# First stage of a hybrid block: x sums in other tiles, normed parts ahead of adds, two splits and two constants moved

## The chip, the cores and the metric

The kernel runs on one core of a Trainium2 chip. The metric is the device time of one execution in microseconds (us). Engines are named as in the profile: PE (TensorE, the matmuls), PEld (its weight loads), DVE (VectorE), ACT (ScalarE), POOL (GpSimd) and SP (SyncE, which here issues most DMAs). Each engine works through its own list of instructions in order, and waits on semaphores for the others. L93 is line 93 of the kernel.

## What is computed

x is 1024 tokens by 1024 channels in float32. A mixer with two branches is followed by a SwiGLU block. Only the second branch is touched by the change:

```python
h = rms_norm(x, norm_mix_g[l])
proj = h @ w_in[l]
rnn_x, rnn_gate, sgu_u, sgu_v, gate_a, gate_b = jnp.split(proj, SPLIT_POINTS, axis=-1)
...
y_b = chunked_sgu(jax.nn.gelu(sgu_u), jax.nn.gelu(sgu_v), sgu_ln_g[l], sgu_ln_b[l], sgu_ws[l], sgu_bs[l])
```

`chunked_sgu` takes a layer norm of gelu(v) over its 1024 channels, multiplies each chunk of 128 tokens by a lower triangular 128x128 matrix for each of 8 groups of channels (the mixing), and multiplies the result by gelu(u). The first branch needs a few constants from `rg_lambda` (8 columns of 128) before its recurrence can run.

## The kernel before

Every float32 product is made of three matmuls with halves of the operands: ACT copies a value into a high half (`split`, L93), DVE subtracts to get the low half (L94), and PE adds hi*hi, hi*lo and lo*hi (L97, L98, L99). The large products are Strassen/Winograd products: seven block products M1 to M7, whose left operands are blocks of x or sums of them (A11, A12, A22, S1 to S4), each split once, and whose right operands are weights loaded to `wraw` and split (b11, b21, b22, and t1 to t4, which are sums formed on DVE by L206 to L217).

The first stage is the projection v with what hangs on it. Its instructions stand on every engine in the order in which the code is written (`tc.manual_schedule`, L554), up to `ms.__exit__`; behind that a scheduler of the framework orders them. Inside, the second half of v's columns runs in a loop over eight tiles t of 128 tokens. For each t, PE forms the tile (24 matmuls); `v_stats` applies gelu on ACT (L648) and takes statistics on DVE (L649, L653); when t closes its norm group (the groups are tile 0, tiles 1 and 2, 3 and 4, 5 and 6, and 7), `v_norm` forms 1/std on DVE (L659 and L390 to L399) and `v_centre` subtracts the mean on ACT (L668). The tile two places behind is then split into its normed parts (`v_split`: hi on ACT L674, lo on DVE L675; the tag `vn` has two buffers), mixed (`v_mix`: PE L686 and L687, then ACT copies the first sum to `mt`, L689; the tag `mt` has four buffers, four are used for each tile), and `v_mixed` adds the two sums on DVE (L695) and stores from `mt` to `mix_d`.

Between these stand the operands for the next products. `sums(i)` forms S1, the block for S3 and the one for S2 in place with three DVE operations over 128x1024 (L540, L541, L542); `sum_s4(i)` forms S4 (L545); `part(name, src, i)` splits half i of an operand, one ACT and one DVE instruction over 128x1024.

After the loop the two products u0 and u1 begin ("heads", one block product at a time, in the order M1, M2, M5, M6, M3, M7, M4), with the mixing of tiles 6 and 7, the splits of S2 and S4 and, by `take`, results evacuated late. Behind the written order, u's results are multiplied by the mixing's (L838 scales and shifts `mix`, L839 applies gelu to u, L841 multiplies), S3 and A22 are split, and u0 and u1 run to their end. Then come the constants of the recurrence (`sp_e`, L869 and L870; the exponential needs another activation table, ACT_TABLE_LOAD) and the products r0, r1, ... of the first branch mixed with u2, u3 and the gates.

Of the kernel before, what the change touches and what calls it, by code (L numbers as in the profile page):

```python
# [8 lines left out]
F32 = mybir.dt.float32  # L9
F32R = mybir.dt.float32r  # L10
I32 = mybir.dt.int32
AF = mybir.ActivationFunctionType
ALU = mybir.AluOpType

P = 128
T = 1024
D = 1024
NT = T // P
NK = D // P
HALF = 512  # L20
# [26 lines left out]
def ts(t):  # L47
    return slice(t * P, (t + 1) * P)
# [3 lines left out]
def block_kernel(ctx: ExitStack, tc: tile.TileContext, a: dict, out: bass.AP):  # L52
    nc = tc.nc
    act, dve, pool, pe = nc.scalar, nc.vector, nc.gpsimd, nc.tensor
# [30 lines left out]
    def ps(name):  # L85
        return psum.tile([P, HALF], F32, name=name, tag="ps")

    def slot(name, shape=(P, 4, 2, HALF), dt=F32R):
        return slots.tile(list(shape), dt, name=name, tag="s")

    def split(hi, lo, src, eng=None):

        act.activation(hi, src, AF.Copy)  # L93
        (eng or dve).tensor_sub(lo, src, hi.bitcast(F32))  # L94
# [14 lines left out]
    def tick():  # L109
        clock[0] += 1  # L110
        for fn in due.pop(clock[0], []):
            fn()
# [240 lines left out]
    for m in DOWN:  # L353
        i = DL[LEFT[m]]
# [57 lines left out]
    def tm_half(acc, name, A, t, ks, free=0, inner={}):  # L412


        for k in ks:
            w = weight((name, k))
            x = A[t // 4][k // 4][:, k % 4, :, ts(t % 4)]
            mm3(acc, x[:, 0], x[:, 1], w[:, 0], w[:, 1], k == 0, k == NK - 1)
            if k < free:
                allow(state["limit"] + 1)  # L420
            if k in inner:
                inner[k]()
# [26 lines left out]
    with tc.tile_pool(name="phv", bufs=1) as wk:  # L449
        ws = wk.tile([P, GROUPS, 2, P], F32R, name="ws")  # L450
        shift = wk.tile([P, GROUPS, P], F32, name="shift", tag="shift")
# [8 lines left out]
        s1s = {}  # L460
# [42 lines left out]
        def scale_x(h, ks):  # L503
            for k in ks:
                dve.scalar_tensor_tensor(F[h][:, k], F[h][:, k], par("mix_g", k), R[h], ALU.mult, ALU.mult)
# [22 lines left out]
        def part(name, src, i):  # L528

            ks = slice(2 * i, 2 * i + 2)  # L530
            if name not in ops:
                ops[name] = slot(f"h_{name}")
            split(ops[name][:, ks, 0], ops[name][:, ks, 1], src)

        def block(h, kh, i):
            return F[h][:, 4 * kh + 2 * i:4 * kh + 2 * i + 2]

        def sums(i):
            s1 = s1s[i] = wk.tile([P, 2, HALF], F32, name=f"xs{i}", tag="shift")
            dve.tensor_add(s1, block(1, 0, i), block(1, 1, i))  # L540
            dve.tensor_sub(block(1, 0, i), block(0, 0, i), block(1, 0, i))  # L541
            dve.tensor_sub(block(0, 0, i), s1, block(0, 0, i))  # L542

        def sum_s4(i):
            dve.tensor_sub(block(0, 1, i), block(0, 1, i), block(0, 0, i))  # L545
# [95 lines left out]
        v1, stats, mvs, vn, mts = {}, {}, {}, {}, {}  # L641
# [4 lines left out]
        def v_stats(t, acc):  # L646
            v1[t] = wk.tile([P, HALF], F32, name=f"vb{t}", tag="vb", bufs=3)
            act.activation(v1[t], acc, AF.Gelu_apprx_tanh, scale=rms[:, t:t + 1])  # L648
            dve.bn_stats(sts[t][:, 1], v1[t])  # L649
            g = group[t]  # L650
            if t == g[0]:
                mvs[t] = wk.tile([P, 3, len(g)], F32, name=f"mv{t}", tag=f"bnmv{len(g)}", bufs=2)
            dve.bn_aggr(mvs[g[0]][:, :2, t - g[0]], sts[t])  # L653

        def v_norm(t):

            g = group[t]
            mv = mvs[g[0]]
            dve.tensor_scalar(mv[:, 2], mv[:, 0], -1.0, None, ALU.mult)  # L659
            y = rstd_early(wk, mv[:, 1], 1.0, f"rv{t}", len(g))  # L660
            for j, u in enumerate(g):
                stats[u] = y[:, j:j + 1]

        def v_centre(t):
            g = group[t]
            for j, u in enumerate(g):
                for src in (v0[u], v1[u]):
                    act.activation(src, src, AF.Identity, bias=mvs[g[0]][:, 2, j:j + 1])  # L668

        def v_split(t):  # L670
            vn[t] = []
            for q, src in enumerate((v0[t], v1[t])):
                x = wk.tile([P, 2, HALF], F32R, name=f"vn{t}{q}", tag="vn", bufs=2)
                act.activation(x[:, 0], src, AF.Identity, scale=stats[t])  # L674
                dve.scalar_tensor_tensor(x[:, 1], src, stats[t], x[:, 0].bitcast(F32), ALU.mult, ALU.subtract)  # L675
                vn[t].append(x)

        def v_mix(t):
            mts[t] = []
            for i in range(4):  # L680
                g = 2 * i
                x = vn[t][i // 2]
                mx = ps(f"mx{t}{i}").rearrange("p (j s t) -> p j s t", j=2, s=2)
                for j in range(2):
                    c = ts((g + j) % 4)
                    pe.matmul(mx[:, j], x[:, 0, c], ws[:, g + j], start=True, stop=False, skip_group_check=True)  # L686
                    pe.matmul(mx[:, j, 0], x[:, 1, c], ws[:, g + j, 0], start=False, stop=True, skip_group_check=True)  # L687
                mt = wk.tile([P, 2, P], F32, name=f"mt{t}{i}", tag="mt", bufs=4)
                act.activation(mt, mx[:, :, 1], AF.Copy)  # L689
                mts[t].append((mt, mx))  # L690

        def v_mixed(t):
            for i, (mt, mx) in enumerate(mts.pop(t)):
                g = 2 * i
                dve.tensor_add(mt, mt, mx[:, :, 0])  # L695
                nc.sync.dma_start(mix_d[i // 2][:, g % 4:g % 4 + 2, ts(t)], mt)

        for t in range(NT):
            acc = ps(f"pv1{t}")
            if t == 0:  # L700
                state["limit"] = 2 * NK
            tm_half(acc, "wv1", H, t, range(NK), free=2 * (t == NT - 1))
            if t > 1:
                v_split(t - 2)
            if t < 2:
                scale_x(1, range(4 * t, 4 * t + 4))
            if 1 <= t < 3:
                part("A11", block(0, 0, t - 1), t - 1)
            if t == 2:
                sums(0)  # L710
            if t == 4:
                part("S1", s1s[0], 0)
                sums(1)
            if t == 5:
                part("S1", s1s[1], 1)
                part("A12", block(0, 1, 0), 0)
            if t == 6:
                part("A12", block(0, 1, 1), 1)
                sum_s4(0)
            if t == 7:  # L720
                sum_s4(1)
            v_stats(t, acc)
            if t == group[t][-1]:
                v_norm(t)
            if t > 1:
                v_mix(t - 2)
                v_mixed(t - 2)
            if t == group[t][-1]:
                v_centre(t)
            tick()  # L730
# [13 lines left out]
        def head(n):  # L744
            next(U[n])
            tick()

        def take(n):
            for fn in postponed[:n]:
                fn()  # L750
            del postponed[:n]

        cur["defer"] = True
        v_split(6)
        head("u0")
        v_mix(6)
        v_mixed(6)
        v_split(7)
        head("u1")
        take(2)  # L760
        head("u0")
# [9 lines left out]
        take(2)  # L771
        part("S4", block(0, 1, 1), 1)
        head("u0")
        head("u1")
        take(2)
        cur["defer"] = False
    ms.__exit__(None, None, None)

    with tc.tile_pool(name="phr", bufs=2) as wk:
# [70 lines left out]
        for fn in results:  # L850
            fn()
        results.clear()
        for i in range(2):
            part("S3", block(1, 0, i), i)
        for i in range(2):
            c = wk.tile([P, 2, HALF], F32, name=f"a22_{i}", tag="rr")
            act.activation(c, block(1, 1, i), AF.Copy)
            s1s[i] = c
        for i in range(2):
            part("A22", s1s[i], i)  # L860
        state["ahead"] = 5
        run(U["u0"], U["u1"])

# [2 lines left out]
        lam = wk.tile([P, 8], F32, name="lam", bufs=1)  # L866
        load(lam, a["lam"])
        sp = {n: wk.tile([P, 8], F32, name=f"sp_{n}", bufs=1) for n in ("e", "z", "z2", "p", "m", "c4", "c8")}
        act.activation(sp["e"], lam, AF.Abs)  # L869
        act.activation(sp["e"], sp["e"], AF.Exp, scale=-1.0)  # L870
        dve.tensor_scalar(sp["z"], sp["e"], 2.0, None, ALU.add)
        dve.reciprocal(sp["z"], sp["z"])
# [448 lines left out]
    for n, m in enumerate(DOWN):  # L1321
        c = m in CHAIN
# [97 lines left out]
```

## Time and profile before

| | |
|---|---|
| three runs, us | 1429.61, 1430.56, 1432.44; median 1430.56 |
| profiled execution, us | 1431.23 |
| its span, us, and mean granted clock | 1429.5; 0.993 |
| instructions | 17233 |
| busy in the span | PE 98%, PEld 81%, DVE 77%, ACT 56%, POOL 5% |

The profiled execution is one run, with its span measured from the first to the last instruction. Times of a row are microseconds from the span's start. A row of a timeline gives the start, the duration, the engine, the line, the operation, what it writes and reads by the program's names, and in brackets how long the engine was idle just before and what ended that. The granted clock is the share of full speed that PE was given.

### The profile page before, as it was taken

The numbers are of one execution on the slowest core, as the hardware profiler recorded it, in microseconds if no ns is written. First come the engines' busy times: TensorE is split into PE (matmuls) and PEld (weight loads), VectorE is DVE, ScalarE is ACT, GpSimd is POOL, SyncE is SP. The second block draws the span as 40 slices with busy tenths as digits, with TensorE's granted clock in tenths as the row PEclk, the third lists the DMA queues.
The fourth block names the chain that finished last, engine by engine and source line by source line (L and its number), as shares of the span: only waits on it lengthen the run. The fifth ranks groups of instructions, "written<-read, shape, count | busy, mean of one in ns | idle before, by whom it ended". The sixth has DMA issues, their size and how long they took to land.

```text
span 1429.5 us, 17233 instructions
## 1 busy us (share of the span) xinstructions
PE 1403.3 (98%) x6216; PEld 1154.9 (81%) x6216; DVE 1097.7 (77%) x1807; ACT 794.0 (56%) x1320; POOL 74.7 (5%) x59
## 2 busy tenths in 40 slices
PE   9998999999999999999999999999999999999997
PEld 7877887788888887788888788888888888888886
DVE  7998999988888887689757776666666665697585
ACT  8467688888889974353443533333333333444454
POOL 0000000000000000000000021111111111000000
PEclk9999999999999999999999999999999999999999
DMA  9323545433333387773611122222322226842342
GB/s 321 137 60 106 203 160 180 168 116 114 114 121 101 109 327 285 262 291 129 220 60 44 74 111 110 111 92 101 110 111 111 96 96 254 331 182 94 110 141 81
DMA packets 73349, 212.45 MB, mean 149 GB/s; under 512 B 6576, under 2 KB 20912, under 8 KB 60720
## 3 DMA queue, kind: packets, MB, share of 16 engines
q1 hardware_dynamic: 73120, 211.32, 41.5%
q8 instruction: 48, 0.79, 0.2%
q14 instruction: 37, 0.30, 0.1%
q10 hardware_dynamic: 144, 0.04, 0.0%
HBM read 148.68 MB, written 62.65 MB: 148 GB/s over the span
## 4 chain that ended last, share of the span: by engine, by line
PE 71%; DVE 12%; ACT 8%; DMA 5%; issue 2%; SPq 1%; DVEq 0%; ACTq 0%; POOLq 0%; POOL 0%
PE f_p L97 10%; PE f_p L99 10%; PE f_p L98 10%; PE d_M L98 5%; PE d_M L99 5%; PE d_M L97 5%; PE g_p L99 2%; PE g_p L98 2%; PE g_p L97 2%; PE po L97 2%; PE po L99 2%; PE po L98 2%; DMA sb<-sgb_d 2%; PE pa_p L97 2%; PE pa_p L98 2%
## 5 line engine op out<-in xcount | busy, mean ns | idle before, releaser
L93 ACT ACTIVATE dl_M<-wraw 128x512 fp32r<-128x512 f32 x77 | 48.6, 631 | 105.0 <-PE d_M L99 92.2
L98 PE MATMUL d_M<-d_M,dl_M 128*128 128x512 f32 x264 | 102.8, 389 | 0.0
L97 PE MATMUL d_M<-d_M,dl_M 128*128 128x512 f32 x264 | 102.7, 389 | 0.0
L99 PE MATMUL d_M<-d_M,dl_M 128*128 128x512 f32 x264 | 102.7, 389 | 0.0
L93 ACT ACTIVATE f_t<-wraw 128x512 fp32r<-128x512 f32 x88 | 55.5, 630 | 84.0 <-PE f_p L99 71.3
L94 DVE TENSOR_TENSOR dl_M<-wraw,dl_M 128x512 fp32r<-128x512 f32 x77 | 54.0, 701 | 51.5 <-ACT dl_M L93 51.3
L94 DVE TENSOR_TENSOR f_t<-wraw,f_t 128x512 fp32r<-128x512 f32 x88 | 71.7, 815 | 23.6 <-ACT f_t L93 22.6
L97 PE MATMUL f_p<-m,f_b 128*128 128x512 f32 x176 | 69.1, 393 | 0.0
L98 PE MATMUL f_p<-m,f_b 128*128 128x512 f32 x176 | 68.9, 392 | 0.0
L99 PE MATMUL f_p<-m,f_b 128*128 128x512 f32 x176 | 68.9, 391 | 0.0
L97 PE MATMUL f_p<-f_S,f_t 128*128 128x512 f32 x176 | 68.5, 389 | 0.0
L98 PE MATMUL f_p<-f_S,f_t 128*128 128x512 f32 x176 | 68.5, 389 | 0.0
L99 PE MATMUL f_p<-f_S,f_t 128*128 128x512 f32 x176 | 68.5, 389 | 0.0
L97 PE MATMUL f_p<-m,f_t 128*128 128x512 f32 x176 | 68.5, 389 | 0.0
L98 PE MATMUL f_p<-m,f_t 128*128 128x512 f32 x176 | 68.5, 389 | 0.0
L99 PE MATMUL f_p<-m,f_t 128*128 128x512 f32 x176 | 68.5, 389 | 0.0
L93 ACT ACTIVATE f_b<-wraw 128x512 fp32r<-128x512 f32 x66 | 41.1, 626 | 36.2 <-PE f_p L99 31.8
L94 DVE TENSOR_TENSOR f_b<-wraw,f_b 128x512 fp32r<-128x512 f32 x66 | 45.4, 687 | 18.8 <-ACT f_b L93 18.1
L98 PEld LDWEIGHTS d_M<-d_M,dl_M 128*128 128x128 f32 x264 | 49.5, 188 | 10.5 <-DVE d_M L94 0.2
L97 PEld LDWEIGHTS d_M<-d_M,dl_M 128*128 128x128 f32 x264 | 49.6, 188 | 10.4
L99 PEld LDWEIGHTS d_M<-d_M,dl_M 128*128 128x128 f32 x264 | 49.6, 188 | 10.1
L206 DVE TENSOR_TENSOR wraw<-wraw 128x512 f32<-128x512 f32 x50 | 53.0, 1060 | 1.0
(506 smaller groups left out, 4219.7 us busy)
## 6 DMA issues: line engine op xcount, KB each, us to landing
wraw<-in_w_gu_dram SPq DMA_DIRECT2D x22, 1024.0 KB, 4.9
wd<-in_w_down_dram SPq DMA_DIRECT2D x11, 1024.0 KB, 8.7
wraw<-in_w_r_dram SPq DMA_DIRECT2D x8, 1024.0 KB, 6.4
wraw<-in_w_g_dram SPq DMA_DIRECT2D x8, 1024.0 KB, 5.0
wraw<-ffs_d SPq DMA_DIRECT2D x8, 1024.0 KB, 5.0
wraw<-ffa_d SPq DMA_DIRECT2D x6, 1024.0 KB, 6.1
xn<-in_x_dram SPq DMA_DIRECT2D x8, 512.0 KB, 9.2
wraw<-in_w_u_dram SPq DMA_DIRECT2D x4, 1024.0 KB, 5.6
```

What stands on the lines that cost most here:

```text
L93: act.activation(hi, src, AF.Copy)
L94: (eng or dve).tensor_sub(lo, src, hi.bitcast(F32))
L97: pe.matmul(o, lh, rh, start=start, stop=False, **kw)
L98: pe.matmul(o, lh, rl, start=False, stop=False, **kw)
L99: pe.matmul(o, ll, rh, start=False, stop=stop, **kw)
L206: dve.tensor_sub(b11, b12, b11)
```

## The change

In the loop, `sums(0)` and `sums(1)` move from tiles 2 and 4 to tiles 3 and 5; the splits of S1 and A12 are made at tiles 4 and 6; `sum_s4(0)` moves from tile 6 to 7, and `sum_s4(1)` behind the mixing of tile 6. The normed parts of tile 6 are made between the mixing of tile 5 and its adds, those of tile 7 between the mixing of tile 6 and its adds. The splits of S3, the copies of A22's block and their splits move from behind the written order into its end, with buffers of other tags. The first operation of the recurrence constants is bound to its place in the program's order.

```diff
--- before.py
+++ after.py
@@ -706,24 +706,22 @@
                 scale_x(1, range(4 * t, 4 * t + 4))
             if 1 <= t < 3:
                 part("A11", block(0, 0, t - 1), t - 1)
-            if t == 2:
-                sums(0)
-            if t == 4:
-                part("S1", s1s[0], 0)
-                sums(1)
-            if t == 5:
-                part("S1", s1s[1], 1)
-                part("A12", block(0, 1, 0), 0)
-            if t == 6:
-                part("A12", block(0, 1, 1), 1)
+
+            if t in (3, 5):
+                sums(t // 4)
+            if t in (4, 6):
+                i = t // 2 - 2
+                part("S1", s1s[i], i)
+                part("A12", block(0, 1, i), i)
+            if t == 7:
                 sum_s4(0)
-            if t == 7:
-                sum_s4(1)
             v_stats(t, acc)
             if t == group[t][-1]:
                 v_norm(t)
             if t > 1:
                 v_mix(t - 2)
+                if t == NT - 1:
+                    v_split(6)
                 v_mixed(t - 2)
             if t == group[t][-1]:
                 v_centre(t)
@@ -751,11 +749,11 @@
             del postponed[:n]
 
         cur["defer"] = True
-        v_split(6)
         head("u0")
         v_mix(6)
+        v_split(7)
         v_mixed(6)
-        v_split(7)
+        sum_s4(1)
         head("u1")
         take(2)
         head("u0")
@@ -771,8 +769,15 @@
         take(2)
         part("S4", block(0, 1, 1), 1)
         head("u0")
+        a22 = [wk.tile([P, 2, HALF], F32, name=f"a22_{i}", tag=("shift", "vn")[i], bufs=1 + i) for i in range(2)]
+        for i in range(2):
+            act.activation(a22[i], block(1, 1, i), AF.Copy)
+        part("S3", block(1, 0, 0), 0)
         head("u1")
+        part("S3", block(1, 0, 1), 1)
         take(2)
+        for i in range(2):
+            part("A22", a22[i], i)
         cur["defer"] = False
     ms.__exit__(None, None, None)
 
@@ -850,14 +855,6 @@
         for fn in results:
             fn()
         results.clear()
-        for i in range(2):
-            part("S3", block(1, 0, i), i)
-        for i in range(2):
-            c = wk.tile([P, 2, HALF], F32, name=f"a22_{i}", tag="rr")
-            act.activation(c, block(1, 1, i), AF.Copy)
-            s1s[i] = c
-        for i in range(2):
-            part("A22", s1s[i], i)
         state["ahead"] = 5
         run(U["u0"], U["u1"])
 
@@ -866,7 +863,8 @@
         lam = wk.tile([P, 8], F32, name="lam", bufs=1)
         load(lam, a["lam"])
         sp = {n: wk.tile([P, 8], F32, name=f"sp_{n}", bufs=1) for n in ("e", "z", "z2", "p", "m", "c4", "c8")}
-        act.activation(sp["e"], lam, AF.Abs)
+
+        tc.keep_in_program_order(act.activation(sp["e"], lam, AF.Abs))
         act.activation(sp["e"], sp["e"], AF.Exp, scale=-1.0)
         dve.tensor_scalar(sp["z"], sp["e"], 2.0, None, ALU.add)
         dve.reciprocal(sp["z"], sp["z"])
```

On DVE, at tiles 2 and 3 (`xs0`, `x0`, `x1`: the sums; `st`: statistics; `rv2`: 1/std of tiles 1 and 2; `mt00`: first add of tile 0; `vn10`, `vn11`: lo halves of tile 1), DVE has before:

```order
L540 TENSOR_TENSOR xs0_780<-x1_130 128x1024
L541 TENSOR_TENSOR x1_130<-x0_129,x1_130 128x1024
L542 TENSOR_TENSOR x0_129<-xs0_780,x0_129 128x1024
L649 BN_STATS st2_443<-vb2_784 128x6
...
L399 SCALAR_TENSOR_TENSOR rv2_789<-rv2_789 128x2
L695 TENSOR_TENSOR mt00_806<-mt00_806,mx00_801 128x256
...
L675 SCALAR_TENSOR_TENSOR vn10_866<-va1_366,rv2_789,vn10_866 128x512
L675 SCALAR_TENSOR_TENSOR vn11_869<-vb1_742,rv2_789,vn11_869 128x512
L649 BN_STATS st3_447<-vb3_872 128x6
```

and after:

```order
L649 BN_STATS st2_443<-vb2_780 128x6
...
L399 SCALAR_TENSOR_TENSOR rv2_785<-rv2_785 128x2
L695 TENSOR_TENSOR mt00_802<-mt00_802,mx00_797 128x256
...
L675 SCALAR_TENSOR_TENSOR vn10_862<-va1_366,rv2_785,vn10_862 128x512
L675 SCALAR_TENSOR_TENSOR vn11_865<-vb1_742,rv2_785,vn11_865 128x512
L540 TENSOR_TENSOR xs0_868<-x1_130 128x1024
L541 TENSOR_TENSOR x1_130<-x0_129,x1_130 128x1024
L542 TENSOR_TENSOR x0_129<-xs0_868,x0_129 128x1024
L649 BN_STATS st3_447<-vb3_872 128x6
```

The three sums leave the place ahead of tile 2's statistics and stand behind the lo halves of tile 1, ahead of tile 3's statistics.

On DVE, at tile 7 and the first heads (`vn60` to `vn71`: lo halves of tiles 6 and 7; `mt50` to `mt63`: adds of tiles 5 and 6; `u0_b21`, `u1_b21`: weights of the second block products), the difference begins behind tile 7's 1/std; before:

```order
L399 SCALAR_TENSOR_TENSOR rv7_1220<-rv7_1220 128x1
L695 TENSOR_TENSOR mt50_1234<-mt50_1234,mx50_1229 128x256
...
L695 TENSOR_TENSOR mt53_1255<-mt53_1255,mx53_1250 128x256
L675 SCALAR_TENSOR_TENSOR vn60_1267<-va6_601,rv6_1124,vn60_1267 128x512
L675 SCALAR_TENSOR_TENSOR vn61_1270<-vb6_1119,rv6_1124,vn61_1270 128x512
L94 TENSOR_TENSOR u0_b21_1273<-wraw4_630,u0_b21_1273 128x512
L94 TENSOR_TENSOR u1_b21_1276<-wraw5_656,u1_b21_1276 128x512
L695 TENSOR_TENSOR mt60_1297<-mt60_1297,mx60_1292 128x256
...
L695 TENSOR_TENSOR mt63_1318<-mt63_1318,mx63_1313 128x256
L675 SCALAR_TENSOR_TENSOR vn70_1328<-va7_660,rv7_1220,vn70_1328 128x512
L675 SCALAR_TENSOR_TENSOR vn71_1331<-vb7_1214,rv7_1220,vn71_1331 128x512
```

and after:

```order
L399 SCALAR_TENSOR_TENSOR rv7_1219<-rv7_1219 128x1
L675 SCALAR_TENSOR_TENSOR vn60_1256<-va6_601,rv6_1123,vn60_1256 128x512
L675 SCALAR_TENSOR_TENSOR vn61_1259<-vb6_1118,rv6_1123,vn61_1259 128x512
L695 TENSOR_TENSOR mt50_1233<-mt50_1233,mx50_1228 128x256
...
L695 TENSOR_TENSOR mt53_1254<-mt53_1254,mx53_1249 128x256
L94 TENSOR_TENSOR u0_b21_1272<-wraw4_630,u0_b21_1272 128x512
L94 TENSOR_TENSOR u1_b21_1275<-wraw5_656,u1_b21_1275 128x512
L675 SCALAR_TENSOR_TENSOR vn70_1319<-va7_660,rv7_1219,vn70_1319 128x512
L675 SCALAR_TENSOR_TENSOR vn71_1322<-vb7_1213,rv7_1219,vn71_1322 128x512
L695 TENSOR_TENSOR mt60_1296<-mt60_1296,mx60_1291 128x256
...
L695 TENSOR_TENSOR mt63_1317<-mt63_1317,mx63_1312 128x256
L545 TENSOR_TENSOR x0_129<-x0_129 128x1024
```

The lo halves of tiles 6 and 7 each move ahead of the four adds of the tile before, and S4's second sum stands behind the adds of tile 6.

On ACT, at the end of u0 and u1 (`u0_u2` to `u1_p1`: gelu of their results; `u0_t4`, `u1_t4`: weights of the last block products; `r0_...`: weights of the next product), before:

```order
L93 ACTIVATE u0_t4_1551<-wraw4_630 128x512
L93 ACTIVATE u1_t4_1557<-wraw5_656 128x512
L839 ACT_TABLE_LOAD
L839 ACTIVATE u0_u2_1506<-u0_u2_1506 128x512
...
L839 ACTIVATE u1_u2_1508<-u1_u2_1508 128x512
L839 ACTIVATE u0_m5_1473<-u0_m5_1473 128x512
L93 ACTIVATE r0_b11_1581<-wraw6_1554 128x512
L839 ACTIVATE u1_m5_1475<-u1_m5_1475 128x512
L839 ACTIVATE u0_p1_1279<-u0_p1_1279 128x512
L93 ACTIVATE r0_t1_1605<-wraw6_1554 128x512
L93 ACTIVATE r0_b22_1630<-wraw6_1554 128x512
L839 ACTIVATE u1_p1_1339<-u1_p1_1339 128x512
```

and after:

```order
L93 ACTIVATE u1_t4_1557<-wraw5_656 128x512
L844 ACTIVATE u0_u2_1515<-u0_u2_1515 128x512
...
L844 ACTIVATE u1_m5_1475<-u1_m5_1475 128x512
L844 ACTIVATE u0_p1_1278<-u0_p1_1278 128x512
L844 ACTIVATE u1_p1_1339<-u1_p1_1339 128x512
L93 ACTIVATE r0_b11_1581<-wraw6_1554 128x512
L93 ACTIVATE r0_t1_1605<-wraw6_1554 128x512
...
L93 ACTIVATE r0_t3_1682<-wraw6_1554 128x512
L867 ACTIVATE sp_e_1707<-lam_1705 128x8
L868 ACT_TABLE_LOAD
L868 ACTIVATE sp_e_1707<-sp_e_1707 128x8
```

The copy of r0's first weights stood between the gelus of `u0_m5` and `u1_m5` and now stands behind all of them; the constants' operation and table load, which stood ahead of `u1_t2` in the middle of u0 and u1, are now behind r0's weights.

## Rows read from the trace of the kernel before

**Rows 1.** The page: busy us, share of the span and instructions of each engine.
```profile
PE 1403.3 (98%) x6216; PEld 1154.9 (81%) x6216; DVE 1097.7 (77%) x1807; ACT 794.0 (56%) x1320; POOL 74.7 (5%) x59
```

**Rows 2.** Waits of PE, 60 to 150 us: total us, times, longest.
```profile
PE u_p L97 <- ACT u_t L93: 2.4, 1, 2.4
PE mx L687 <- DVE vn L675: 1.9, 3, 1.2
PE mx L686 <- ACT vn L674: 1.3, 1, 1.3
```

**Rows 3.** Stretches of 5 us: busy us (instructions) by engine, granted clock, DMA share, GB/s.
```profile
80.00:85.00 5.00, 4.63 (x22) 4.06 (x23) 3.08 (x8) 2.58 (x7) 0.00 (x0) 0.71 0.56 162
...
120.00:125.00 5.00, 5.00 (x19) 4.16 (x19) 4.60 (x10) 2.79 (x7) 0.00 (x0) 0.69 0.36 107
```

**Rows 4.** The same columns: first stage to the seam, and after it.
```profile
71.50:160.00 88.50, 82.80 (x395) 68.38 (x394) 79.50 (x161) 63.14 (x111) 0.10 (x1) 0.94 0.31 96
160.00:264.20 104.20, 103.24 (x452) 84.30 (x450) 100.31 (x176) 78.67 (x117) 0.20 (x2) 1.00 0.57 189
```

**Rows 5.** Timeline of PE: start, duration, line, operands, [idle before <- releaser].
```profile
163.88 0.39 PE L97 MATMUL r_p<-h_A,r_b 128*128 128x512 f32 x1
...
264.94 0.50 PE L99 MATMUL r_p<-h_A,r_t 128*128 128x512 f32 x1 [1.24 <-DVE r_t L94]
```

**Rows 6.** Timeline of DVE at tiles 2 and 7.
```profile
71.50 1.22 DVE L540 TENSOR_TENSOR xs<-x 128x1024 f32<-128x1024 f32 x1
...
75.16 0.69 DVE L649 BATCH_NORM_STATS2 st<-vb 128x6 f32<-128x512 f32 x1
...
116.43 1.42 DVE L695 TENSOR_TENSOR mt<-mt,mx 128x256 f32<-128x256 f32 x4
117.76 0.75 DVE L675 SCALAR_TENSOR_TENSOR vn<-va,rv,vn 128x512 fp32r<-128x512 f32 x1
```

**Rows 7.** Waits of DVE, 71.5 to 160 us.
```profile
DVE mt L695 <- ACT mt L689: 3.1, 3, 1.9
DVE h_S L94 <- ACT h_S L93: 2.2, 4, 1.2
DVE u_t L94 <- ACT u_t L93: 1.0, 1, 1.0
DVE vn L675 <- ACT vn L674: 0.4, 2, 0.2
```

**Rows 8.** Timeline of ACT: the copy of mt that waits for a store.
```profile
84.25 0.38 ACT L689 ACTIVATE mt<-mx 128x256 f32<-128x256 f32 x1 [1.99 <-DMA mix_d<-mt]
```

**Rows 9.** Timeline of ACT around u1's end.
```profile
158.38 0.63 ACT L93 ACTIVATE r_b<-wraw 128x512 fp32r<-128x512 f32 x1 [1.10 <-DMA wraw<-in_w_r_dram]
...
164.08 0.58 ACT L839 ACTIVATE u_p<-u_p 128x512 f32<-128x512 f32 x1 [1.08 <-PE u_p L99]
```

**Rows 10.** Timeline of DVE around u1's end.
```profile
159.46 0.69 DVE L94 TENSOR_TENSOR r_b<-wraw,r_b 128x512 fp32r<-128x512 f32 x1
```

**Rows 11.** Timeline of ACT: the recurrence constants.
```profile
140.51 0.21 ACT L869 ACTIVATE sp_e<-lam 128x8 f32<-128x8 f32 x1 [1.28 <-DMA lam<-in_lam_dram]
140.74 1.28 ACT L870 ACT_TABLE_LOAD   x1
142.03 0.21 ACT L870 ACTIVATE sp_e<-sp_e 128x8 f32<-128x8 f32 x1
```

**Rows 12.** Waits of DVE, 160 to 264.2 us.
```profile
DVE mix L838 <- DMA mix<-mix_d: 1.3, 1, 1.3
DVE th L955 <- ACT gt L948: 0.8, 1, 0.8
DVE gt L949 <- ACT gt L940: 0.5, 1, 0.5
DVE xc L918 <- ACT xc L916: 0.3, 1, 0.3
DVE xs L94 <- ACT xs L93: 0.3, 1, 0.3
```

## The prediction

> **What bounds the kernel now.** I read four views, from coarse to fine. First the busy shares [rows 1]: TensorE (PE) is busy 98% of the span, so the end can only move by what PE loses in waits or half clock, and by what something else makes PE wait for. Then PE's waits in the stretch that the change touches [rows 2]: 5.6 us in five waits, 3.2 of them in the mixing (1.3 for ScalarE's normed part, 1.9 for VectorE's) and 2.4 once, for a hi half that ScalarE copies late. Each long wait is followed by a stretch at the lower of the two clock levels: the granted clock is 0.71 in 80 to 85 us and 0.69 in 120 to 125 [rows 3], which at 1.2 instead of 2.4 GHz costs about 5 x 0.3 = 1.5 us each, 1.7 with the edges that fall in the neighbouring windows. A third, after the 2.4 us wait, I put at the same price.
>
> That reads as if PE's waits were all there is to win. The windows by engine say otherwise [rows 4]. From 160 to 264.2 us VectorE (DVE) is busy 100.31 of 104.2 us, 96%. At the end of that stretch, at 264.94, PE stands 1.24 us and waits for a lo half that DVE subtracts (tile r_t, the fourth weight sum of r2) [rows 5]. The subtraction starts the moment DVE comes to it. So up to there PE has slack and DVE has none. The work that DVE has ahead of this subtraction is the same set of instructions before and after the change, only in another order. The shift of the end is therefore, first, the difference in DVE's idle time between 71.5 and 264 us, and not the difference in PE's. I do the sum on DVE.
>
> **The change, part by part.**
>
> *The x sums one tile later.* At tile 2 three DVE operations over 128x1024 stand from 71.50 to 75.16, 3.66 us, ahead of tile 2's statistics [rows 6], and the norm, the adds and the lo halves of tile 1 all queue behind them. Moved behind tile 1's lo halves they leave this path: the mixing of tile 1 then finds its parts (my estimate from the same durations: 77.6 against 78.1 when PE comes), the wait of 1.3 and the piece of 0.4 behind it go, and with them the dip. For PE that is 1.7 + 1.7 = 3.4. For DVE nothing is removed, but its longest wait for a copy mt (1.9 of the 3.1 in [rows 7]) is now covered by the sums: -1.9 of idle. That copy is late in the kernel before because ScalarE waits 1.99 us for the store of an older mt, whose buffer it takes [rows 8]. Should the sums not cover it, the 1.9 stays.
>
> *Normed parts of tiles 6 and 7 ahead of adds.* The four adds of tile 5 take 1.33 (116.43 to 117.76) and stand ahead of tile 6's lo halves [rows 6]; in the new order the lo halves come first, so PE's wait of 1.2 in the mixing of tile 6 falls to about 0.6, and the dip behind it (1.7) may go. The price: the adds, and so the stores of tile 5, are late relative to the mixing of tile 6, whose four copies need the same four mt buffers. I put the adds' end at 115.7, the last landing at 118.4, the last copy at 118.8. Tile 7's two ScalarE parts stand behind that copy on ScalarE, and DVE now has tile 7's lo halves ahead of tile 6's adds: it stands from 116.9 to 119.5, about 2.65 of new idle. From below this is 0 (stores land as copies come), from above 4 (the wait of [rows 8] doubled). I take 2.65.
>
> *S3 and A22 in the v stage.* The same four 128x1024 splits and two copies, earlier by several places. ScalarE becomes the one to wait for: in my estimate DVE stands 0.3 + 0.8 + 1.75 = 2.85 behind hi halves there, in place of the waits for h_S and u_t (2.2 + 1.0) [rows 7]. The two scale-adds and multiplies of the u results that filled such gaps are pushed back, 2.5 us of DVE work, to after u1.
>
> *What stands at the seam to the next stage.* In the kernel before, ScalarE's hi copy of r0's first weights runs at 158.38, as soon as the load is in, ahead of the last gelu of u1, which at 164.08 waits for u1's last matmul [rows 9]. DVE's lo half follows at 159.46 [rows 10] and PE starts r0 at 163.88 without waiting [rows 5]. In the new order the copy stands behind that gelu. So PE can't begin r0 when it ends u1: gelu 0.58, copy 0.5, subtraction 0.6 come between, about 1.65 of PE wait, and DVE, whose pushed-back work is queued behind the subtraction, stands about 2.9. From below 0 (if it had other work queued), from above 4.6, if PE's dip at u1's M6 holds u1's end up by 1.7.
>
> *Recurrence constants later.* One table load leaves the stretch before u1's second product, where ScalarE had a 1.28 load in front of a hi half that PE waited 2.4 us for [rows 2, 11]. That gain is PE's. ScalarE's list has two table loads more up to the first gate, one for the constants and one back: 2 x 1.28 = 2.57. ScalarE is idle a quarter of 160 to 264 us (78.67 of 104.2 busy [rows 4]) so these are mostly hidden: 0 taken, 2.57 for the range.
>
> A rule from the Trainium skill (ScalarE: Activation LUTs, What ACT_TABLE_LOAD costs) puts a switch of table at 1.28 us for the load and 1.38 us of drain, 2.66 in all. The row shows the 1.28 and nothing of the drain: the operation before ends at 140.72, the load stands at 140.74, the next operation at 142.03 [rows 11]. By the page two more loads would be an estimated 5.3 us of ScalarE, by the row 2.57; if the page held, the slower rival's far end below would lie 2.7 later.
>
> *The sum, on DVE.* Idle of before up to the seam 6.7 (3.1 + 2.2 + 1.0 + 0.4, [rows 7]); after 2.65 + 2.85 + 2.9 = 8.4. So DVE comes out of the seam 1.7 later in its work. From there to 264 the kernel before has 3.2 of waits [rows 12], of which 1.3 is for a DMA and the rest for ScalarE; a DVE that is late finds these already served. Between none and all I take half: -1.6. A dip at u1's M6 (PE still waits about 2 there) would add 1.7; at even odds 0.8. 1.7 - 1.6 + 0.8 = +0.9. The profiled execution (span 1429.5, its own time 1431.23) lies 0.67 above the median of the runs, 1430.56; the shift goes on the median: 1431.5. For PE alone I find it 5.3 ahead when u1 ends, but by this sum it spends that waiting at r0 and at r2.
>
> **The rivals.**
>
> *A, forecast: DVE's ledger evens out*, +0.9, 1431.5; within it everything from all waits recovered (1.7 - 3.3 = -1.6) to none but no dip or half of one (+2.6): 1429.0 to 1433.2.
>
> *B, faster: PE's savings stay.* If the copy of r0's weights is not what DVE stands for at the seam (the 2.9 falls away), and the later waits are recovered too: -1.6 - 2.9 = -4.5, 1426.1; the most that PE can keep is its 5.3, 1425.3. For it: PE stands only 1.24 at r2, so little recovery on DVE is enough to make PE the bound again. Against it: 96% busy DVE, and an order in which the copy does stand behind the gelu.
>
> *C, slower: the seam.* r0's first hi copy waits behind u1's last gelu, u1 runs through a dip, PE's wait at r0 is long enough for the clock to fall again, and nothing comes back later: 1.7 + 1.7 = 3.4, with one of the two table loads on the path 4.7, with both 6.0: 1434.0 to 1436.5, taken at 1435.3. It decides when DVE is over 3 us late out of the seam. For it: ScalarE's list. Against: 3.2 of recoverable waits.
>
> *D, the adds' late stores don't delay anything* (the 2.65 is 0): then DVE is 1.7 - 2.65 = -1 out of the seam and -2.6 at r2: 1428, between A and B, and I count it with whichever it falls to.
>
> **How the numbers follow.** A difference under 0.2%, 2.9 us, can't be told from none: the bounds are 1427.7 and 1433.4. A has 0.45, B with D's far half 0.27, C 0.28. Range: from B's 1426.1, widened little, to between C's value and its far end: 1426.3 to 1436.0. A's own range is 1429.0 to 1433.2.
>
> **What would show it right or wrong.** Right, step by step: no wait of PE for tile 1's mixing and granted clock 1.0 in 80 to 85; a DVE wait of 2 to 3 us ahead of tile 7's lo halves; PE's first matmul of r0 waiting 1 to 2 us for a DVE lo half, its hi copy right behind u1's last gelu; PE at r2's product waiting for DVE still, and the end shifted by as much as that subtraction. Wrong: r2's product shifted by -3 or more with PE not waiting there (B), or the last part of the kernel, after 264 us, with another length than before, since I let everything behind r2 shift as one block.

## The result, and the profile after

| | before | changed |
|---|---|---|
| median of six runs, us | 1430.67 | 1438.91 |
| profiled execution, span, us | 1429.5 | 1435.1 |
| ratio | 1 | 1.0054, 95% interval 1.0041 to 1.0068 |

The changed kernel is 0.54% slower, about 7.7 us, beyond the far end of the slower rival. PE's busy time is 1.9 us less than in [rows 1], so the loss lies in waits:

```profile
span 1435.1 us, 17236 instructions
...
PE 1401.4 (98%) x6216; PEld 1152.5 (80%) x6216; DVE 1098.0 (77%) x1807; ACT 795.7 (55%) x1322; POOL 74.7 (5%) x59
```

PE's waits from 60 to 300 us in the changed kernel (engine, line, what it waited for: total us, times, longest) answer to [rows 2]:

```profile
PE r_p L97 <- ACT r_y L233: 4.5, 1, 4.5
PE r_p L97 <- ACT r_b L93: 4.5, 1, 4.5
PE u_p L97 <- DVE mt L695: 1.7, 1, 1.7
PE r_p L99 <- DVE r_t L94: 1.2, 1, 1.2
PE u_p L97 <- ACT u_t L93: 1.2, 1, 1.2
PE mx L687 <- DVE vn L675: 0.8, 2, 0.6
```

The mixing's waits have fallen from 3.2 to 0.8 us, as the change wants, against a new one of 1.7 for tile 6's adds (`mt`, L695). But two waits of 4.5 stand at the head of r0, which the kernel before doesn't have at all: one for the hi half of r0's first weights (`r_b`), one for the evacuation of r0's first sum (`r_y`). The windows (busy us by engine, granted clock, DMA share, GB/s) answer to [rows 3]:

```profile
80.00:85.00 5.00, 5.00 (x23) 4.10 (x22) 4.96 (x10) 3.51 (x5) 0.00 (x0) 1.00 0.30 88
120.00:125.00 5.00, 5.00 (x32) 4.40 (x31) 4.96 (x10) 1.53 (x3) 0.00 (x0) 1.00 0.38 109
...
135.00:140.00 5.00, 3.85 (x16) 2.54 (x16) 3.98 (x6) 4.30 (x7) 0.00 (x0) 1.00 0.00 0
140.00:145.00 5.00, 5.00 (x24) 4.14 (x23) 3.39 (x4) 5.00 (x8) 0.00 (x0) 1.00 0.00 0
...
160.00:165.00 5.00, 4.05 (x10) 3.14 (x11) 3.97 (x6) 1.78 (x3) 0.00 (x0) 0.50 0.91 292
...
175.00:180.00 5.00, 5.00 (x14) 3.92 (x13) 5.00 (x14) 0.96 (x3) 0.00 (x0) 0.56 0.86 305
```

The clock is at its full 1.00 at 80 and 120 us, where it was 0.71 and 0.69. In the stretches behind the two new waits it is 0.50, which is the lower level of 1.2 GHz, and 0.56, most of it at that level.

What holds r0 up isn't an engine. SyncE (SP) waits once for 19.5 us, and this is the longest wait of its queue from 100 to 185 us:

```profile
SPq L436 <- DVE h_A L94: 19.5, 1, 19.5
```

It waits for a lo half of A22, the last on DVE's timeline of the written order:

```profile
148.93 1.22 DVE L94 TENSOR_TENSOR h_A<-a,h_A 128x1024 fp32r<-128x1024 f32 x1
```

Right behind it, SP's timeline shows the loads of the next stage go out (`x4` and `x2` are rows that the view joins, the duration covering their waits):

```profile
150.28 0.33 SPq L436 DMA_DIRECT2D mix<-mix_d  x1
150.66 0.43 SPq L436 DMA_DIRECT2D sh<-shift_d  x1
...
152.08 0.43 SPq L133 DMA_DIRECT2D wraw<-in_w_r_dram  x1
155.20 4.12 SPq L439 DMA_DIRECT2D yb_d_A<-u_y  x2
159.37 0.43 SPq L133 DMA_DIRECT2D wraw<-in_w_u_dram  x1
159.84 3.01 SPq L436 DMA_DIRECT2D mix<-mix_d  x4
162.90 0.71 SPq L436 DMA_DIRECT2D lam<-in_lam_dram  x1
```

The first load of `mix` goes out at 150.28; before, it went out at 133.68:

```profile
133.68 0.33 SPq L436 DMA_DIRECT2D mix<-mix_d  x1
...
153.54 0.33 SPq L133 DMA_DIRECT2D wraw<-in_w_r_dram  x1
```

The loads that stand behind it in SP's queue go out right after it. For r0's weights (`in_w_r`) that isn't late: they leave at 152.08, 1.5 us earlier than before. What is late is their landing, and PE needs them earlier. They leave in a crowd of `mix` and `sh` loads and land after 8.2 us, where the kernel before had 4.8, and PE ends u1 7.4 us earlier than before. With 4.8 us they would have landed some 3.3 earlier, which leaves about 1.2 of the wait of 4.5 (an estimate from these rows). That the crowd makes the landing slow is argued, from a run below in which the weights leave at the same time without the crowd. The stores of `u_y` need a product with `mix`, so SP stands at them until 159, and the four loads of `mix` behind them go out from 159.84 to 162.85; the constants' `lam` follows. ScalarE's timeline shows both consequences:

```profile
156.47 0.58 ACT L844 ACTIVATE u_p<-u_p 128x512 f32<-128x512 f32 x1 [2.14 <-PE u_p L99]
160.26 0.63 ACT L93 ACTIVATE r_b<-wraw 128x512 fp32r<-128x512 f32 x1 [3.21 <-DMA wraw<-in_w_r_dram]
...
169.61 0.21 ACT L867 ACTIVATE sp_e<-lam 128x8 f32<-128x8 f32 x1 [2.84 <-issue]
169.84 1.28 ACT L868 ACT_TABLE_LOAD   x1
171.13 0.21 ACT L868 ACTIVATE sp_e<-sp_e 128x8 f32<-128x8 f32 x1
173.28 0.60 ACT L233 ACTIVATE r_y<-r_p 128x512 f32<-128x512 f32 x1 [1.94 <-DVE yb_s L815]
```

The copy of r0's weights at 160.26 waits 3.21 for the load, and answers to [rows 9]: u1's last gelu, which the prediction put in its way, is long over. PE's own row gives r0's start:

```profile
160.95 0.79 PE L97 MATMUL r_p<-h_A,r_b 128*128 128x512 f32 x1 [4.51 <-ACT r_b L93]
```

The copy of r0's first sum comes at 173.28, for it needs one of six buffers that u0's and u1's results hold until they have been multiplied by `mix` and added (DVE `yb_s`).

### The profile page after: what moved, and what is told of

Its sections match the earlier page's. It is cut to its first block, busy times and chain, and to the rows that moved or that the text cites. A ratio compares the mean times of both kernels' runs of the same rounds, so it can differ in the third digit from the quotient of the medians.

```text
span 1435.1 us, 17236 instructions
## 1 busy us (share of the span) xinstructions
PE 1401.4 (98%) x6216; PEld 1152.5 (80%) x6216; DVE 1098.0 (77%) x1807; ACT 795.7 (55%) x1322; POOL 74.7 (5%) x59
## 4 chain that ended last, share of the span: by engine, by line
PE 74%; DVE 11%; ACT 8%; DMA 4%; issue 2%; SPq 0%; DVEq 0%; ACTq 0%; POOL 0%; POOLq 0%
PE f_p L98 10%; PE f_p L99 10%; PE f_p L97 10%; PE d_M L97 5%; PE d_M L99 5%; PE d_M L98 5%; PE g_p L99 2%; PE g_p L97 2%; PE g_p L98 2%; PE po L99 2%; PE po L97 2%; PE po L98 2%; DMA sb<-sgb_d 2%; PE pa_p L97 2%; PE pa_p L98 2%
```

## The experiments

Each ratio is against runs of the kernel before on the same chip; -1% is about 14.3 us.

| run | ratio | 95% interval | us against before |
|---|---|---|---|
| changed | 1.0054 | 1.0041 to 1.0068 | +7.7 |
| S3 and A22 back | 0.9968 | 0.9957 to 0.9979 | -4.6 |
| S3 and A22 alone | 1.0044 | 1.0030 to 1.0058 | +6.3 |
| A22 back | 0.9978 | 0.9967 to 0.9989 | -3.1 |
| sums and normed parts only | 0.9965 | 0.9952 to 0.9978 | -5.0 |
| one late reader | 1.0014 | 1.0004 to 1.0023 | +2.0 |
| more work on DVE | 1.0021 | 1.0010 to 1.0032 | +3.0 |
| sums alone | 0.9980 | 0.9971 to 0.9989 | -2.9 |
| normed parts alone | 0.9990 | 0.9980 to 0.9999 | -1.4 |
| A22 read elsewhere | 0.9977 | 0.9967 to 0.9986 | -3.3 |
| tile 6 only | 0.9957 | 0.9945 to 0.9969 | -6.2 |
| five mt buffers | 0.9956 | 0.9944 to 0.9968 | -6.3 |
| tile 6 only, five mt buffers | 0.9946 | 0.9934 to 0.9959 | -7.7 |

(us = (ratio - 1) x 1431.)

**S3 and A22 back.** Changed kernel, without its third part:

```diff
-        a22 = [wk.tile([P, 2, HALF], F32, name=f"a22_{i}", tag=("shift", "vn")[i], bufs=1 + i) for i in range(2)]
-        for i in range(2):
-            act.activation(a22[i], block(1, 1, i), AF.Copy)
-        part("S3", block(1, 0, 0), 0)
         head("u1")
-        part("S3", block(1, 0, 1), 1)
         take(2)
-        for i in range(2):
-            part("A22", a22[i], i)
...
```

Behind the written order these parts then stand as in the kernel before.

> The changed kernel with the splits of S3 and A22 and A22's copies back behind the written order. Theory M (memory): the loads behind the first stage use the memory that the stage gives up when its last reader is done, and the last reader in the changed kernel is A22's last lo half at 150; with S3 and A22 back, SP issues the first mix load at 125 to 129 us (133.7 before, 150.3 changed), PE has no wait of 4.5 at r0, and the time is below before: 1423 to 1428. Rival O (order on ScalarE and VectorE, the ledger of the prediction): the loss comes from the reordered sums and normed parts and from the constants; 1432 to 1439 here too, with a PE wait of over 1 us at r0.

Measured 0.9968: the loss turns into a gain. SP's timeline has the first `mix` load and r0's weights early, the load 2 us behind the expected 125 to 129:

```profile
131.03 0.33 SPq L436 DMA_DIRECT2D mix<-mix_d  x1
...
148.37 0.33 SPq L133 DMA_DIRECT2D wraw<-in_w_r_dram  x1
```

PE has no wait at r0. So the first two parts of the change, and the constants, are worth 4.6 us; the third costs 12.3 on top of them.

**S3 and A22 alone.** The kernel before, with the third part only (the diff above the other way round):

> The kernel before with only the splits of S3 and A22 moved into the written order. Theory M: the first mix load waits for A22's last lo half, near 155 us, and PE waits at r0 for the loads behind it: 1437 to 1443. Rival O: within 2 us of before, 1429 to 1433, since neither sums nor normed parts nor constants moved.

Measured 1.0044, +6.3: the loss comes without any of the other parts. SP's wait is there too (its first `mix` load goes out at 150.04), and so are PE's two at r0:

```profile
SPq L436 <- DVE h_A L94: 18.6, 1, 18.6
...
PE r_p L97 <- ACT r_y L233: 5.3, 1, 5.3
PE r_p L97 <- ACT r_b L93: 3.5, 1, 3.5
```

**A22 back.** The changed kernel with S3's splits in the written order and A22's copies and splits behind it:

```diff
         part("S3", block(1, 0, 0), 0)
         head("u1")
         part("S3", block(1, 0, 1), 1)
         take(2)
-        for i in range(2):
-            part("A22", a22[i], i)
```

> The changed kernel with S3 split in the written order, but A22's copies and splits back behind it: S3's split reads and writes no memory of the first stage's pool. Theory M: as the run with both back, first mix load at 125 to 130 us, no wait at r0, 1423 to 1429. If instead it is ScalarE's fuller list at the stage's end that counts (rival O): 1435 to 1440.

Measured 0.9978. S3 early costs 1.4 of the 12.3, which the intervals can't tell from nothing; A22 is the rest. PE's wait at r0 is 0.4, and there is one of 2.7 at the gates that the kernel with both back doesn't have. Here r0's weights leave when they do in the changed kernel, but the first loads of `mix` and `sh` have been out since 131, and the copy follows after 4.9 us and not 8.2 (SP's and ScalarE's timelines):

```profile
152.15 0.33 SPq L133 DMA_DIRECT2D wraw<-in_w_r_dram  x1
...
157.04 0.63 ACT L93 ACTIVATE r_b<-wraw 128x512 fp32r<-128x512 f32 x1 [1.36 <-DMA wraw<-in_w_r_dram]
```

**One late reader.** The kernel of the first experiment, with one more DVE instruction, on one element per partition:

```diff
         head("u1")
         take(2)
+        dve.tensor_scalar(s1s[1][:, 0, :1], s1s[1][:, 0, :1], 1.0, None, ALU.mult)
         cur["defer"] = False
```

> The kernel with S3 and A22 back (sums, normed parts and constants as changed), and one DVE operation on a column of one element per partition of the first stage's memory (the buffer of xs1) as the last thing written in the first stage; it multiplies by one. Theory M: that alone holds SP's first mix load from 131 to where the last DVE operation of the written order runs, 142 to 148 us, and PE waits 2 to 5 us at r0: 1430 to 1438, over 3 above the kernel without it (1427.0). Rival: the splits of A22 themselves, 2.4 us of DVE and 4 of ScalarE earlier, cost what was lost; then one small operation changes nothing, 1426 to 1428.

Measured 1.0014, 6.6 us above the kernel without it (1.0014 / 0.9968). SP's first load waits for that instruction:

```profile
SPq L436 <- DVE xs L774: 11.0, 1, 11.0
```

The load goes out at 142.50 and not at 131.03. What I expected at r0 came elsewhere: the loads are 8 us earlier than in the changed kernel, PE has no wait at r0 for its weights, and waits at u1 and at the first gates instead:

```profile
PE pgt L97 <- ACT xs L93: 3.4, 2, 2.7
...
PE u_p L99 <- DVE u_t L94: 1.5, 1, 1.5
PE u_p L97 <- DVE u_m L242: 1.5, 1, 1.5
```

The waits at the gates are no mark of the late load: A22 back has 2.7 there and the next run 2.6, with the first load out at 131. The two of 1.5 at u1 stand in neither of them.

**A22 read elsewhere.** The changed kernel's four A22 instructions in their place, but fed from A11 and without copies in the first stage's memory:

```diff
-        a22 = [wk.tile([P, 2, HALF], F32, name=f"a22_{i}", tag=("shift", "vn")[i], bufs=1 + i) for i in range(2)]
-        for i in range(2):
-            act.activation(a22[i], block(1, 1, i), AF.Copy)
...
-            part("A22", a22[i], i)
+            part("A22", ops["A11"][:, 2 * i:2 * i + 2, 0].bitcast(F32), i)
```

> The changed kernel with A22's four split instructions where the change puts them, but with no copy in the first stage's memory: they read A11's high halves in place of A22's block, and the two copies on ScalarE are left out (so A22 holds other numbers; the rest of the work is the same). Theory M: nothing of the first stage's memory is read late, the first mix load goes out at 129 to 132 us, no wait of 4.5 at r0, 1425 to 1429. Rival: the splits' early place on ScalarE and VectorE is what costs: 1435 to 1439, less 1 for the copies.

Measured 0.9977, as with A22 back, 11 us below the changed kernel. SP's timeline:

```profile
130.76 0.33 SPq L436 DMA_DIRECT2D mix<-mix_d  x1
...
133.51 0.43 SPq L436 DMA_DIRECT2D lam<-in_lam_dram  x1
...
153.45 0.33 SPq L133 DMA_DIRECT2D wraw<-in_w_r_dram  x1
```

The splits' place costs nothing that the runs can tell (0.9977, and 0.9978 with A22 back); the memory that their source lies in does. Two copies of about 1 us each on ScalarE are missing here and can't be told apart from that, but the late reader has shown 6.6 us without any of them.

One thing these runs don't hold still is the order behind the written stage, which the framework's scheduler sets for each of them. In the changed kernel and with S3 and A22 alone, SP's list has r0's weights as the fifth transfer of the new stage, ahead of `lam` and four loads of `mix`; in the kernel before and in the other runs of this kind they are the twelfth. So the 11 to 12 us are the price of the late reader together with the order that the scheduler makes of it. One comparison is cleaner: one late reader, A22 back and A22 read elsewhere have the same 22 transfers in the same order on SP up to 170 us, and the late reader is 5.2 us slower than either (1.0014 against 0.9978 and 0.9977). ScalarE's and DVE's orders differ there too.

**The other parts.** The recurrence constants as before (sums and normed parts only), the sums alone, and the normed parts alone:

> The kernel before with the sums and the normed parts moved, S3, A22 and the recurrence constants as before. Theory M: 1423 to 1429, within 2 us of the run that also has the constants later. Rival O: 1431 to 1436.

> The kernel before with the x sums, S1, A12 and S4's sums moved alone. Theory M with PE's stalls of the v stage: the 1.7 of wait and the 1.7 of half clock at tile 1 go, 1427 to 1429. Prediction's ledger: VectorE's 1.9 of idle goes, half of it kept: 1429 to 1431.

> The kernel before with the normed parts of tiles 6 and 7 ahead of the adds alone. PE's wait of 1.2 and its half clock at tile 6 go or shrink, 1428 to 1430; by the prediction's ledger VectorE's new wait of 2.4 ahead of tile 7's lo halves shows in the end: 1431 to 1434.

```diff
+            if t in (3, 5):
+                sums(t // 4)
+            if t in (4, 6):
+                i = t // 2 - 2
+                part("S1", s1s[i], i)
+                part("A12", block(0, 1, i), i)
...
+                if t == NT - 1:
+                    v_split(6)
                 v_mixed(t - 2)
```

Down to the dots these lines belong to the sums, below them to the normed parts. Measured -2.9 for the sums and -1.4 for the normed parts, -5.0 together, -4.6 with the constants later: the two add up, and the constants' place makes no difference that these runs can tell. The prediction's ledger expected the normed parts alone to be slower; they aren't.

**More work on DVE.** The first experiment's kernel and 8 DVE operations more in the first recurrence, to test whether DVE paces the stretch:

```diff
                     dve.tensor_scalar(q[h], q[h], -1.0, 1.0, ALU.mult, ALU.add)
+                    for _ in range(4 if f == 0 else 0):
+                        dve.tensor_scalar(q[h], q[h], 1.0, None, ALU.mult)
```

> The kernel with S3 and A22 back, and 8 more DVE operations of 128x512 (multiply by one, about 0.4 us each, 3.3 in all) in the recurrence of the first channel tile, near 190 us. If VectorE paces the stretch up to r2, as the prediction has it: 2.5 to 3.5 us later, 1429.5 to 1430.5. If VectorE only follows PE there with slack: under 1 us, 1426.5 to 1428.

Measured 1.0021, 7.6 us above the kernel without them, over twice the work added. It is inconclusive: the framework's scheduler put the instructions behind it in another order, and over half of it is one new wait of PE at the gates:

```profile
PE pgt L97 <- ACT xs L93: 4.3, 1, 4.3
```

**Towards a better one.** In the changed kernel DVE stands 2.35 us ahead of tile 7's lo halves, since ScalarE waits for stores of mt. The experiments leave the constants, S3 and A22 as before, and move tile 7's normed parts back, or give mt a fifth buffer, or both:

```diff
         v_mix(6)
-        v_split(7)
         v_mixed(6)
+        v_split(7)
         sum_s4(1)
...
-                mt = wk.tile([P, 2, P], F32, name=f"mt{t}{i}", tag="mt", bufs=4)
+                mt = wk.tile([P, 2, P], F32, name=f"mt{t}{i}", tag="mt", bufs=5)
```

> Sums moved and tile 6's normed parts ahead of tile 5's adds, tile 7's as in the kernel before (behind tile 6's adds). VectorE's wait of 2.4 ahead of tile 7's lo halves should fall under 0.5, and the mixing of tile 7 start up to 1 us later. If that wait matters to the end: 1424 to 1426; if only PE's own stalls do: 1426 to 1428, as with both moved (1426.5).

> Sums and both normed parts moved, and a fifth buffer for mt. ScalarE's wait for a store of mt falls from 2.2 to 1 or less, VectorE's wait of 2.4 by as much: 1425 to 1426.5 if it matters, the same 1426.5 if not.

> Tile 6's normed parts alone moved with the sums, and five buffers for mt: the sum of both small gains at most, 1423.5 to 1426.5.

Measured 0.9957, 0.9956 and 0.9946. Each alone is about 1.2 us below the 0.9965 of the sums and normed parts, within the intervals; both together 2.7, where the intervals still overlap a little, with a median of 1423.61. What the traces show of the reason differs from what was expected. With tile 6's parts only, DVE's wait ahead of tile 7's lo halves falls to 0.19 and PE's wait for tile 6's adds from 1.7 to 0.4. The fifth buffer takes ScalarE's wait for a store only from 2.2 to 1.9, and DVE's to 1.88. This version beats the kernel before by 7.7 us and the changed one by 15. PE's waits in it (60 to 300 us):

```profile
PE u_p L97 <- ACT u_t L93: 1.7, 1, 1.7
PE r_p L99 <- DVE r_t L94: 1.2, 1, 1.2
PE mx L687 <- DVE vn L675: 0.8, 2, 0.6
```

## Why the prediction was wrong

It forecast no change and the kernel is slower. The step that failed is in the part on S3 and A22: "the same four 128x1024 splits and two copies, earlier by several places". I priced it as 2.85 us of DVE behind ScalarE and 2.5 of DVE work pushed back, and that is not where the loss is. I counted what the instructions do to the engines and not what their buffers hold. The copies took buffers of the first stage (the tags `shift` and `vn`), and A22's splits became that memory's last readers, at 150 us. The loads of the next stage go into the same memory, so the first of them waited for that, and SP's queue with it. SP's waits of 19.5, 18.6 and 11.0 us show this, and so do the times: with the memory left out of it (A22 read elsewhere) the loss goes, and with one small late reader 6.6 us come back. How the loss divides between the wait itself and the scheduler's other order behind it isn't shown. Whether the wait comes from the very bytes or from the stage's memory as a whole was not tried; the same load waits for a reader of a `vn` buffer (the second copy of A22) in one run and of an `xs` buffer in another, which speaks for the whole. The prediction has no term for SP's queue at all: the part asks what is late on ScalarE, DVE and PE, and not what the queue's first row after the stage waits for.

The other steps, in the prediction's order:

- *The sums one tile later*: right. No wait for tile 1's mixing, full clock at 80 us; alone -2.9 us, which is near the 3.4 given for PE.
- *The normed parts*: right in size. DVE stands 2.35 ahead of tile 7's lo halves (2.65 predicted), first row below. Their price for PE, 1.7 of wait for tile 6's adds, had no term. That they would cost more than they bring was wrong: alone they gain 1.4. Whether DVE's idle time shows in the end at all isn't settled, for the run without it (tile 6 only) is 1.1 faster, within the intervals.
- *ScalarE as the one to wait for behind S4, A22 and S3*: right, 0.26 + 0.69 + 1.61 = 2.56 in the rows below, 2.85 predicted. But DVE then stood 3.7 more for `sh`, which is one of the late loads. DVE's timeline in the changed kernel answers to [rows 6, 7]:

```profile
118.95 0.75 DVE L675 SCALAR_TENSOR_TENSOR vn<-va,rv,vn 128x512 fp32r<-128x512 f32 x1 [2.35 <-ACT vn L674]
...
137.76 1.23 DVE L94 TENSOR_TENSOR h_S<-x,h_S 128x1024 fp32r<-128x1024 f32 x1 [0.26 <-ACT h_S L93]
139.68 1.23 DVE L94 TENSOR_TENSOR h_S<-x,h_S 128x1024 fp32r<-128x1024 f32 x1 [0.69 <-ACT h_S L93]
142.52 1.22 DVE L94 TENSOR_TENSOR h_S<-x,h_S 128x1024 fp32r<-128x1024 f32 x1 [1.61 <-ACT h_S L93]
```

- *The seam*: a wait at r0 of 1.65 was predicted for an order on ScalarE, and there is one of 4.51, for a load that lands late and a PE that comes early. The copy behind the gelu, on which rival C rested, cost nothing. The wait's place was right, its cause and size weren't.
- *The second wait of 4.55* and its half clock had no term. The two waits, 9.1 us, and at most 5 x 0.50 + 5 x 0.44 = 4.7 for the half clock behind them (an estimate from the windows above) come to about the 13.2 by which the rows at r2 below lie apart (271.43 - 258.19).
- *The dip at u1's M6*, at even odds, didn't come: PE waits 1.15 there and the clock stays at 1.00 (the windows of 135 and 140 us above).
- *The constants*: no cost, as taken. In the changed kernel they stand on ScalarE until 169.61, when `lam`, issued at 162.90, has landed 6.6 later, but what releases the copy behind them is DVE at 173. The rows above show the table load of 1.28 at 169.84, right behind the operation that ends at 169.82, and the next operation at 171.13. The Trainium skill (ScalarE: Activation LUTs, What ACT_TABLE_LOAD costs) adds a drain of 1.38 to such a load; these rows, like those of [rows 11], show none.
- *The sum on DVE.* Here the prediction has an error that the net result hides. I held that PE would spend its lead, put at 5.3, waiting at r0 and r2. PE ends u1 at 156.44 in the changed kernel (160.95 - 4.51), 7.4 ahead of 163.88 in [rows 5]. With S3 and A22 back such a lead is kept: PE starts r0 at 157.58, 6.30 ahead of [rows 5], and r2's matmul comes at 258.19, 6.75 ahead, with the same wait of 1.24 for DVE. (That profiled execution, 1422.79, is the fastest of its eight.)

```profile
157.58 0.39 PE L97 MATMUL r_p<-h_A,r_b 128*128 128x512 f32 x1
...
258.19 0.50 PE L99 MATMUL r_p<-h_A,r_t 128*128 128x512 f32 x1 [1.24 <-DVE r_t L94]
```

In the changed kernel the same row stands 6.5 later than before, with the same 1.24 again:

```profile
271.43 0.50 PE L99 MATMUL r_p<-h_A,r_t 128*128 128x512 f32 x1 [1.24 <-DVE r_t L94]
```

So the wait at r2 does not say that DVE has a fixed amount of work to get through from 71 us on; DVE comes earlier or later with PE and with the loads. The other traces bear this out. In the kernel before and in seven others (S3 and A22 back, sums and normed parts only, sums alone, normed parts alone, and the three of the better version) r0 starts anywhere from 155.38 to 163.88, and this matmul of r2 follows 100.4 to 101.1 us later, with a wait of 1.24 to 1.26. (With A22 back and A22 read elsewhere, which have the waits at the gates, the stretch is 2 to 3 us longer.) PE is busy in nearly all of that time (103.24 of 104.2 us in [rows 4]). The last part of the kernel did shift as one block, as assumed: behind this matmul there are 1164.6 us before and 1163.7 in the changed kernel. The window up to 160 us with S3 and A22 back answers to [rows 4]:

```profile
71.50:160.00 88.50, 83.88 (x423) 69.93 (x423) 83.59 (x170) 63.68 (x114) 0.10 (x1) 1.00 0.36 110
```

Of 88.5 us it now works 83.59 and not 79.50: of the waits in [rows 7], the 3.1 for `mt`, the 1.0 for `u_t` and 1.9 of the 2.2 for `h_S` are gone. (The ledger put the idle time before at 6.7; the window in [rows 4] has 9.0.) Rival B was right for the first two parts of the change. Whether DVE could hold up the stretch from r0 to r2 stays open, since the experiment that added DVE work also changed the order; that it would eat up PE's lead, as the ledger has it, happened in none of these eight traces.

## What to carry to other kernels

When work moves into a stage, ask what its buffers hold back: here the next stage's first load waited for the last reader of the memory that the stage gave up, and the loads behind it in that DMA queue waited with it. Look up in the trace what the queue's first row after the move waits for, before summing engine time. And an engine's idle time in one trace is no fixed sum: take away a stall of PE, and the waits of the engines that feed it shrink with it.

## What the runs showed of the hardware that I had not expected

A wait of PE alone doesn't tell whether its clock falls. In the kernel before, waits of 1.3, 1.2 and 2.4 us were each followed by a stretch at 1.2 GHz (granted clock 0.50 from 83 to 85, 120 to 123 and 144 to 147 us). In the changed kernel waits of 1.65 and 1.15 weren't, and with one late reader PE, with two waits of 1.5, was busy 2.48 of 5 us and stayed at 1.00 in that stretch and the next (windows as above):

```profile
150.00:155.00 5.00, 2.48 (x10) 1.75 (x11) 5.00 (x9) 0.84 (x2) 0.00 (x0) 1.00 0.56 147
155.00:160.00 5.00, 5.00 (x24) 4.12 (x23) 4.52 (x8) 1.85 (x3) 0.00 (x0) 1.00 0.93 321
```

This is one execution, and the fastest of twelve: its mean granted clock is 0.998, and the other eleven have 0.993 to 0.996 and take 1431.3 to 1436.2 us. So the same kernel can run with falls of the clock that this trace doesn't have. Where they come, and whether behind these waits, isn't shown.
